# Three of the seven up products with the high and low rows in one 512-column matmul

## The chip, the cores and the metric

The kernel runs on one core of a Trainium2 chip. The metric is device time in microseconds (us): the median of 3 runs for the kernel before. Profiles come from one profiled execution each.

## The reference, cut to what matters

The reference is one decoder block: two mixing branches, and then a gated ConvFFN on 512 tokens. The change touches only the first product of the ConvFFN:

```python
def conv_ffn(h, w_up, conv_w, conv_b, w_down):
    u = h @ w_up                                  # 512 x 2048 @ 2048 x 11264, float32
    ...
    c = up[:, 0:S] * conv_w[0] + up[:, 1:S + 1] * conv_w[1] + up[:, 2:S + 2] * conv_w[2] + conv_b
    val, gate = jnp.split(c, 2, axis=-1)
    return (jax.nn.silu(gate) * val) @ w_down
```

## The kernel before

**Products.** A float32 operand is split into a high part and a low part (type fp32r), and a product is taken as three matmuls: high weights by high rows, high weights by low rows, low weights by high rows. `h @ w_up` is done in 44 blocks `f`. Block `f` gives 128 channels of the value half and 128 of the gate half, for all 512 tokens. It is a 2 by 2 by 2 block product (channel half, half of the 2048 inputs, half of the tokens), done with seven products instead of eight: P1, P2, P7, P6, P5, Q4, P3. Each product multiplies a 1024 x 128 weight tile (a tile of `w_up`, or a sum of such tiles) by 1024 x 256 rows. The rows, sums of quarters of `h`, are prepared once and stay in SBUF as high and low tiles: b11, b21, b22, t1, t2, t3, t4, each 128 x 8 x 256.

**One product (`mm`, L1109).** For each of 8 slices k of the inputs, three matmuls of 256 columns go into one PSUM accumulator (L1124): `whi` by the high rows, `whi` by the low rows, `wlo` by the high rows, so 24 matmuls a product and 168 a block. There are three accumulators a block: X, Y and Z. A PSUM bank holds 512 columns; from block 4 on each accumulator has a bank for itself and uses its first 256 columns. X takes P1, P6, P5, P3, Y takes P7 and Q4, Z takes P2.

**Preparing weights (`load`, `sums`, `parts`).** SyncE loads the tiles, and for some a GpSimd DMA adds a second tile to the one in SBUF (L1093). For P6 and P3 VectorE adds two tiles first (L1100). ScalarE copies the tile to the high part `whi` (L1105), VectorE subtracts it for the low part `wlo` (L1107). The ring for `whi` and `wlo` holds three products.

**Taking out (`out`, L1127).** ScalarE copies X into `u` (L1152) after P1, P6, P5 and P3. VectorE adds Z into `u` after P2 (L1156), Y after Q4 (L1156), and Y after P5 (L1154, behind ScalarE's copy of X).

**Behind it.** `conv` (L1161) puts the convolution, silu and gating into a list `later`: ScalarE L1173 and L1179, VectorE L1176 and L1181. After an odd block VectorE also makes factors for the down product (L884 to L888), and ScalarE issues their stores (L893 to L895).

**Order of the work.** From block 7 on the steps of a block are P7, P6, P2, P5, P1 of the next block, Q4, P3; the last block has P6, P7, P5, P2, Q4, P3. At step i, `run` (L1252) first prepares the weights of step i + 2 with one entry of `later` beside it, then emits the matmuls of step i and then its `out`. All of these instructions are pinned to this order on each engine, and each engine runs its list in order.

Of the kernel before, what the change touches and what calls it, by code (L numbers as in the profile page):

```python
# [8 lines left out]
F32 = mybir.dt.float32  # L9
F32R = mybir.dt.float32r  # L10
# [3 lines left out]
ALU = mybir.AluOpType  # L14
# [4 lines left out]
P = 128  # L19
S = 512  # L20
# [114 lines left out]
def block_kernel(ctx: ExitStack, tc: tile.TileContext, d: Dims, a: dict, out: bass.AP):  # L135
    nc = tc.nc
    act, dve, pool, pe, sync = nc.scalar, nc.vector, nc.gpsimd, nc.tensor, nc.sync
    NK, NP, NQ, NKV, NF = d.NK, d.NP, d.NQ, d.NKV, d.NF
# [16 lines left out]
    NPRE = 4  # L155
# [50 lines left out]
    pin = tc.keep_in_program_order  # L206
# [13 lines left out]
    for f in range(NPRE):  # L220
        w, t = a["w_up"][f], {n: up_d[f, n] for n in ("s3", "s1", "P6", "P3")}
# [70 lines left out]
    if True:  # L292
# [3 lines left out]
        with tc.tile_pool(name="x0_ps", bufs=6, space=PSUM) as ps0:  # L296
# [10 lines left out]
            for h in range(2):  # L307
                hs = slice(h * HT * P, (h + 1) * HT * P)
                for k in range(NK):
                    ps = ps0.tile([P, HT * P], F32, name="ps_x", tag="x")  # L310
# [45 lines left out]
        with ExitStack() as pt:  # L356
# [32 lines left out]
            for t in range(NKV):  # L389
# [12 lines left out]
                ps = small().rearrange("p (n c) -> p n c", c=P)  # L402
                for b in range(NT):
                    pe.transpose(ps[:, b], vf[:, b * P : (b + 1) * P], ident)
                ps = ps.rearrange("p n (h c) -> p n h c", c=HD)
# [14 lines left out]
            for g in range(NHK):  # L420
# [7 lines left out]
                for n in range(NT):  # L428
# [37 lines left out]
                    ps = small()  # L466
# [540 lines left out]

    upx = ExitStack()
    bqp = upx.enter_context(tc.tile_pool(name="bqA", bufs=1, reuse_waits="tile"))
    bq = {n: [bqp.tile([P, KH, TH], F32R, name=f"{n}{i}") for i in range(2)] for n in ("b11", "b21")}  # L1010
    hp = hps.enter_context(tc.tile_pool(name="hhlO", bufs=3, reuse_waits="tile"))
    NCC = d.D // S
    ssp = tcp.tile([P, NT, NCC], F32, name="ssp")
# [62 lines left out]
    us = []  # L1076
    dve.tensor_scalar(cw[:, 0:3, NF:], cw[:, 0:3, NF:], -1.0, None, op0=ALU.mult)

    class Block:

        def __init__(self, f):
            self.f, self.w, self.hl = f, {}, {}
            self.apart = 2 <= f < NPRE

        def load(self, n):
            f, w = self.f, self.w
# [20 lines left out]
        def mm(self, n):  # L1109
            if n == "P1":  # L1110
                x = ups.tile([P, S], F32, name="X", tag="X")
                self.X = x[:, :TH]
                self.Z = x[:, TH:] if self.f < NPRE else upy.tile([P, S], F32, name="Z", tag="Y")[:, :TH]
            if n == "P7":
                self.Y = upy.tile([P, S], F32, name="Y", tag="Y")[:, :TH]
            into = {"P2": "Z", "P7": "Y", "Q4": "Y"}.get(n, "X")
            ps = getattr(self, "Z" if self.apart and n in ("P5", "P3") else into)
            start = n in ("P1", "P7") or n == "P2" and self.f >= NPRE or n == "P5" and self.apart
            whi, wlo = (x.rearrange("p (k c) -> p k c", c=P) for x in self.hl.pop(n))
            xh, xl = bq[{"P1": "b11", "P2": "b21", "P7": "t3", "P6": "t2", "P5": "t1", "Q4": "t4", "P3": "b22"}[n]]  # L1120
            for k in range(KH):
                last = k == KH - 1
                for i, (l, r) in enumerate(((whi, xh), (whi, xl), (wlo, xh))):
                    pin(pe.matmul(ps, l[:, k], r[:, k], start=start and k + i == 0, stop=last and i == 2,  # L1124
                                  skip_group_check=True))

        def out(self, n):  # L1127
            if n == "P7":
                return
            X, Y, Z = self.X, getattr(self, "Y", None), self.Z  # L1130
            if n == "P1" and self.f < NPRE:
                self.t1 = up.tile([P, TH], F32, name="t1", tag="t1", bufs=NPRE)
                pin(act.activation(self.t1, X, AF.Copy))
                return

            if self.f < NPRE:
                if n == "P2":
                    pin(dve.tensor_tensor(self.t1, self.t1, Z, op=ALU.add))
                    return
                if self.apart and n != "P1":  # L1140
                    if n != "P6":
                        i, j, more = {"P5": (1, 1, (Z, Y)), "P3": (0, 1, (Z,)), "Q4": (1, 0, (Y,))}[n]
                        u = us[self.f % 2][:, i, 2 + j * TH : 2 + (j + 1) * TH]
                        pin(act.activation(u, X, AF.Copy))
                        for ps in more:
                            pin(dve.tensor_tensor(u, u, ps, op=ALU.add))
                    return
            i, j, ps, first = {"P1": (0, 0, X, True), "P2": (0, 0, Z, False), "P6": (1, 0, X, True), "P5": (1, 1, X, True),
                               "Q4": (1, 0, Y, False), "P3": (0, 1, X, True)}[n]
            u = us[self.f % 2][:, i, 2 + j * TH : 2 + (j + 1) * TH]  # L1150
            if first:
                pin(act.activation(u, ps, AF.Copy))  # L1152
                if n == "P5":
                    pin(dve.tensor_tensor(u, u, Y, op=ALU.add))  # L1154
            else:
                pin(dve.tensor_tensor(u, u, ps, op=ALU.add))  # L1156

        def place(self):
            pin(act.activation(us[self.f % 2][:, 0, 2 : 2 + TH], self.t1, AF.Copy))
# [137 lines left out]


    bqp = upx.enter_context(tc.tile_pool(name="bqB", bufs=1, reuse_waits="tile"))
    bq.update({n: [bqp.tile([P, KH, TH], F32R, name=f"{n}{i}") for i in range(2)] for n in ("b22", "t1", "t3", "t2", "t4")})  # L1300
    up = upx.enter_context(tc.tile_pool(name="upw", bufs=1, side="left", reuse_waits="tile"))

    psx = ExitStack()
# [180 lines left out]
```

## Time and profile before

| what | value |
| --- | --- |
| median of 3 runs (lowest to highest) | 2802.57 us (2802.53 to 2804.05) |
| the profiled execution's own time | 2802.24 us |
| its span, first to last instruction | 2800.5 us |
| mean granted TensorE clock | 0.998 |
| VectorE busy, whole span | 71% |
| ScalarE busy, whole span | 48% |
| up blocks, first and last matmul start | 1474.6 to about 2376 us of the span |

Engines in the profile: PE is TensorE's matmuls, PEld its weight loads, DVE is VectorE, ACT ScalarE, POOL GpSimd, SP SyncE. L1124 is line 1124 of the kernel. A row of the timeline gives start, duration, engine, line, operation, output<-inputs and count, and in brackets how long the engine sat idle before it and what ended that. Durations of neighbours on one engine overlap, so the spacing of starts tells how long an instruction holds its engine.

### The profile page before, as it was taken

The page shows a single profiled execution, that of the slowest core. Times are in us where ns is not written, and L with a number is a line of the kernel's source. Part 1 is how long each engine was busy: PE and PEld are TensorE (multiplying, and loading weights), DVE is VectorE, ACT ScalarE, POOL GpSimd, SP SyncE. Part 2 cuts the span into 40 slices and gives each one's busy share as a digit, 9 for nine tenths or more (in the row PEclk, how much of TensorE's full clock was granted, in tenths as well). Part 3 has the DMA queues.
Part 4 walks back from the last instruction along what each step waited for, and adds up shares of the span by engine and source line. Part 5 has one row for each costly group of instructions (what it writes and reads, how often), then busy time and mean ns, then how long its engine had stood idle before and what let it go on. Part 6 is the DMA issues. An engine that isn't in the chain of part 4 may idle for free.

```text
span 2800.5 us, 45992 instructions
## 1 busy us (share of the span) xinstructions
PE 2759.3 (99%) x17466; PEld 2400.8 (86%) x17466; DVE 1988.9 (71%) x3452; ACT 1352.9 (48%) x2278; POOL 231.3 (8%) x307
## 2 busy tenths in 40 slices
PE   6999999999999999999999999999999999999999
PEld 5777778787778778888889999999999999888887
DVE  5588677877787774545678778787777778655555
ACT  4255445545544553322465555554555555444444
POOL 0001011110111001011000011101010101000000
PEclk9999999999999999999999999999999999999999
DMA  7865887787778767888776888888898888877775
GB/s 221 226 160 161 210 212 187 189 195 192 186 184 198 183 176 216 243 250 283 252 256 186 233 227 227 243 232 222 232 243 229 225 231 237 319 243 240 257 256 187
DMA packets 227182, 619.62 MB, mean 221 GB/s; under 512 B 24832, under 2 KB 44944, under 8 KB 225936
## 3 DMA queue, kind: packets, MB, share of 16 engines
q1 hardware_dynamic: 158400, 441.03, 48.2%
q0 software_dynamic: 37216, 136.33, 25.7%
q10 hardware_dynamic: 31344, 39.31, 4.1%
q8 instruction: 137, 2.24, 0.3%
q14 instruction: 85, 0.70, 0.1%
HBM read 566.96 MB, written 191.18 MB: 271 GB/s over the span
## 4 chain that ended last, share of the span: by engine, by line
PE 63%; DVE 2%; DMA 1%; ACT 1%; issue 0%; ACTq 0%; DVEq 0%; SPq 0%
PE X L1124 17%; PE X L988 10%; PE Y L988 9%; PE Y L1124 9%; PE acc L270 4%; PE acc L269 4%; PE acc L271 4%; PE Z L1124 4%; DMA raw<-in_w_dn_dram 1%; DVE wlo L1107 0%; DVE c L1176 0%; PE psS L761 0%; ACT whi L1105 0%; PE ps_t L1054 0%; PE psG L752 0%
## 5 line engine op out<-in xcount | busy, mean ns | idle before, releaser
L269 PE MATMUL acc<-xhi,whi 128*128 128x512 f32 x1152 | 462.7, 402 | 1.9 <-DVE xlo L315 1.9
L270 PE MATMUL acc<-xlo,whi 128*128 128x512 f32 x1152 | 459.8, 399 | 0.0
L271 PE MATMUL acc<-xhi,wlo 128*128 128x512 f32 x1152 | 459.5, 399 | 0.0
L254 ACT ACTIVATE whi<-raw 128x512 fp32r<-128x512 f32 x352 | 220.5, 630 | 404.9 <-PE acc L270 326.6
L981 DVE TENSOR_TENSOR wlo<-raw,whi 128x1024 fp32r<-128x1024 f32 x210 | 256.7, 1224 | 199.7 <-ACT whi L980 198.2
L980 ACT ACTIVATE whi<-raw 128x1024 fp32r<-128x1024 f32 x210 | 222.5, 1060 | 282.2 <-PE X L988 131.9
L255 DVE TENSOR_TENSOR wlo<-raw,whi 128x512 fp32r<-128x512 f32 x352 | 241.7, 689 | 162.3 <-ACT whi L254 142.7
L1107 DVE TENSOR_TENSOR wlo<-raw,whi 128x1024 fp32r<-128x1024 f32 x184 | 224.6, 1222 | 77.4 <-ACT whi L1105 77.3
L1124 PE MATMUL X<-b,whi 128*128 128x256 f32 x1472 | 268.9, 283 | 0.2 <-ACT whi L1105 0.2
L1124 PE MATMUL X<-t,whi 128*128 128x256 f32 x1408 | 257.2, 283 | 1.4 <-ACT u L1152 1.4
L1124 PE MATMUL Y<-t,whi 128*128 128x256 f32 x1408 | 257.1, 283 | 0.0
L269 PEld LDWEIGHTS acc<-xhi,whi 128*128 128x128 f32 x1152 | 217.0, 188 | 41.7 <-DVE xlo L315 2.1
L271 PEld LDWEIGHTS acc<-xhi,wlo 128*128 128x128 f32 x1152 | 216.8, 188 | 40.0 <-issue 0.9
L270 PEld LDWEIGHTS acc<-xlo,whi 128*128 128x128 f32 x1152 | 217.0, 188 | 39.4 <-issue 1.7
L1124 PEld LDWEIGHTS X<-b,whi 128*128 128x128 f32 x1472 | 229.6, 192 | 0.5 <-ACT whi L1105 0.4
L1105 ACT ACTIVATE whi<-a 128x1024 fp32r<-128x1024 f32 x124 | 130.9, 1056 | 201.3 <-DVE a L1100 195.9
L1124 PEld LDWEIGHTS X<-t,whi 128*128 128x128 f32 x1408 | 219.6, 192 | 1.6 <-ACT u L1152 1.6
L1124 PEld LDWEIGHTS Y<-t,whi 128*128 128x128 f32 x1408 | 219.6, 192 | 0.0
L1124 PE MATMUL X<-b,wlo 128*128 128x256 f32 x736 | 208.5, 283 | 0.9 <-DVE wlo L1107 0.9
L1105 ACT ACTIVATE whi<-raw 128x1024 fp32r<-128x1024 f32 x184 | 192.9, 1049 | 23.0 <-ACT whi L1105 13.9
L1107 DVE TENSOR_TENSOR wlo<-a,whi 128x1024 fp32r<-128x1024 f32 x124 | 151.9, 1225 | 67.6 <-ACT whi L1105 67.0
L1124 PE MATMUL X<-t,wlo 128*128 128x256 f32 x704 | 199.4, 283 | 0.3 <-DVE wlo L1107 0.3
(387 smaller groups left out, 5796.9 us busy)
## 6 DMA issues: line engine op xcount, KB each, us to landing
raw<-in_w_up_dram SPq DMA_DIRECT2D x170, 512.0 KB
raw<-in_w_z_dram SPq DMA_DIRECT2D x288, 256.0 KB
s_dn<-in_w_dn_dram POOLq DMA_DIRECT2D x88, 512.0 KB, 7.4
raw<-s_dn SPq DMA_DIRECT2D x88, 512.0 KB
raw<-in_w_up_dram POOLq DMA_DIRECT2D x80, 512.0 KB, 8.5
raw<-in_w_dn_dram SPq DMA_DIRECT2D x66, 512.0 KB
s_dn<-in_w_dn_dram SPq DMA_DIRECT2D x44, 512.0 KB
s_dn<-s_dn SPq DMA_DIRECT2D x44, 512.0 KB
```

Of the source, the lines that this page charges most:

```text
L254: act.activation(hi, raw, AF.Copy)
L255: dve.tensor_tensor(lo, raw, hi.bitcast(F32), op=ALU.subtract)
L269: stream.append(pe.matmul(acc, whi[:, j], xhi[:, k], start=first, stop=False))
L270: stream.append(pe.matmul(acc, whi[:, j], xlo[:, k], start=False, stop=False))
L271: stream.append(pe.matmul(acc, wlo[:, j], xhi[:, k], start=False, stop=last))
L980: act.activation(whi, wr, AF.Copy)
L981: dve.tensor_tensor(wlo, wr, whi.bitcast(F32), op=ALU.subtract)
L988: pe.matmul(dst, l[:, q, ts], r[:, es], start=fst and j == 0, stop=lst and j == 2, skip_group_check=True)
L1105: pin(act.activation(hi, t, AF.Copy))
L1107: return lambda: pin(dve.tensor_tensor(lo, t, hi.bitcast(F32), op=ALU.subtract))
L1124: pin(pe.matmul(ps, l[:, k], r[:, k], start=start and k + i == 0, stop=last and i == 2, skip_group_check=True))
```

## The change

High and low rows of one name now lie in one tile (`bqt`), high first. In blocks 7 to 42, the products P7, Q4 and P2 pass both in one matmul of 512 columns: high weights by (high rows, low rows). It writes a whole PSUM bank; the first 256 columns get high by high, the other 256 high by low. `wlo` by the high rows still goes to the first 256 columns. So the low sums of Y and of Z stand in the second half of the bank, and `out` adds them into `u` with one more VectorE add after P5, Q4 and P2 each.

```diff
--- before.py
+++ after.py
@@ -1007,7 +1007,8 @@
 
     upx = ExitStack()
     bqp = upx.enter_context(tc.tile_pool(name="bqA", bufs=1, reuse_waits="tile"))
-    bq = {n: [bqp.tile([P, KH, TH], F32R, name=f"{n}{i}") for i in range(2)] for n in ("b11", "b21")}
+    bqt = {n: bqp.tile([P, 2, KH, TH], F32R, name=n) for n in ("b11", "b21")}
+    bq = {n: [t[:, i] for i in range(2)] for n, t in bqt.items()}
     hp = hps.enter_context(tc.tile_pool(name="hhlO", bufs=3, reuse_waits="tile"))
     NCC = d.D // S
     ssp = tcp.tile([P, NT, NCC], F32, name="ssp")
@@ -1076,13 +1077,16 @@
     us = []
     dve.tensor_scalar(cw[:, 0:3, NF:], cw[:, 0:3, NF:], -1.0, None, op0=ALU.mult)
 
+    WIDE = ("P7", "Q4", "P2")
+
     class Block:
 
 
 
         def __init__(self, f):
-            self.f, self.w, self.hl = f, {}, {}
+            self.f, self.w, self.hl, self.full = f, {}, {}, {}
             self.apart = 2 <= f < NPRE
+            self.wide = WIDE if NPRE + 3 <= f < NF - 1 else ()
 
         def load(self, n):
             f, w = self.f, self.w
@@ -1110,16 +1114,26 @@
             if n == "P1":
                 x = ups.tile([P, S], F32, name="X", tag="X")
                 self.X = x[:, :TH]
-                self.Z = x[:, TH:] if self.f < NPRE else upy.tile([P, S], F32, name="Z", tag="Y")[:, :TH]
+                z = x if self.f < NPRE else upy.tile([P, S], F32, name="Z", tag="Y")
+                self.Z = x[:, TH:] if self.f < NPRE else z[:, :TH]
+                self.full.update(X=x.rearrange("p (e s) -> p e s", e=2), Z=z.rearrange("p (e s) -> p e s", e=2))
             if n == "P7":
-                self.Y = upy.tile([P, S], F32, name="Y", tag="Y")[:, :TH]
+                y = upy.tile([P, S], F32, name="Y", tag="Y")
+                self.Y = y[:, :TH]
+                self.full["Y"] = y.rearrange("p (e s) -> p e s", e=2)
             into = {"P2": "Z", "P7": "Y", "Q4": "Y"}.get(n, "X")
             ps = getattr(self, "Z" if self.apart and n in ("P5", "P3") else into)
             start = n in ("P1", "P7") or n == "P2" and self.f >= NPRE or n == "P5" and self.apart
             whi, wlo = (x.rearrange("p (k c) -> p k c", c=P) for x in self.hl.pop(n))
-            xh, xl = bq[{"P1": "b11", "P2": "b21", "P7": "t3", "P6": "t2", "P5": "t1", "Q4": "t4", "P3": "b22"}[n]]
+            nm = {"P1": "b11", "P2": "b21", "P7": "t3", "P6": "t2", "P5": "t1", "Q4": "t4", "P3": "b22"}[n]
+            xh, xl = bq[nm]
             for k in range(KH):
                 last = k == KH - 1
+                if n in self.wide:
+                    pin(pe.matmul(self.full[into], whi[:, k], bqt[nm][:, :, k], start=start and k == 0, stop=False,
+                                  skip_group_check=True))
+                    pin(pe.matmul(ps, wlo[:, k], xh[:, k], start=False, stop=last, skip_group_check=True))
+                    continue
                 for i, (l, r) in enumerate(((whi, xh), (whi, xl), (wlo, xh))):
                     pin(pe.matmul(ps, l[:, k], r[:, k], start=start and k + i == 0, stop=last and i == 2,
                                   skip_group_check=True))
@@ -1148,12 +1162,16 @@
             i, j, ps, first = {"P1": (0, 0, X, True), "P2": (0, 0, Z, False), "P6": (1, 0, X, True), "P5": (1, 1, X, True),
                                "Q4": (1, 0, Y, False), "P3": (0, 1, X, True)}[n]
             u = us[self.f % 2][:, i, 2 + j * TH : 2 + (j + 1) * TH]
+            adds = [Y] if n == "P5" else []
+            adds += [self.full["Y"][:, 1]] if n in ("P5", "Q4") and "P7" in self.wide else []
+            adds += [self.full["Z"][:, 1]] if n == "P2" and n in self.wide else []
+            adds += [self.full["X"][:, 1]] if n in ("P5", "P3") and n in self.wide else []
             if first:
                 pin(act.activation(u, ps, AF.Copy))
-                if n == "P5":
-                    pin(dve.tensor_tensor(u, u, Y, op=ALU.add))
             else:
-                pin(dve.tensor_tensor(u, u, ps, op=ALU.add))
+                adds.insert(0, ps)
+            for more in adds:
+                pin(dve.tensor_tensor(u, u, more, op=ALU.add))
 
         def place(self):
             pin(act.activation(us[self.f % 2][:, 0, 2 : 2 + TH], self.t1, AF.Copy))
@@ -1297,7 +1315,8 @@
 
 
     bqp = upx.enter_context(tc.tile_pool(name="bqB", bufs=1, reuse_waits="tile"))
-    bq.update({n: [bqp.tile([P, KH, TH], F32R, name=f"{n}{i}") for i in range(2)] for n in ("b22", "t1", "t3", "t2", "t4")})
+    bqt.update({n: bqp.tile([P, 2, KH, TH], F32R, name=n) for n in ("b22", "t1", "t3", "t2", "t4")})
+    bq.update({n: [t[:, i] for i in range(2)] for n, t in bqt.items()})
     up = upx.enter_context(tc.tile_pool(name="upw", bufs=1, side="left", reuse_waits="tile"))
 
     psx = ExitStack()
```

`order` of the built programs shows what this makes on the engines. In all, PE has 864 matmuls fewer (24 in each of 36 blocks) and VectorE 108 adds more; the lists of ScalarE, GpSimd and SyncE hold the same instructions.

PE, the start of P2 in a steady block, before (b_13704 and b_13705 are the high and low rows b21; the brackets name the engines whose semaphore is waited for):

```order
L1124 MATMUL Z<-b_13704,whi 128x256 [waits Activation_49]
L1124 MATMUL Z<-b_13705,whi 128x256
L1124 MATMUL Z<-b_13704,wlo 128x256 [waits DVE_49]
L1124 MATMUL Z<-b_13704,whi 128x256
L1124 MATMUL Z<-b_13705,whi 128x256
L1124 MATMUL Z<-b_13704,wlo 128x256
```

The same place in the change, with one tile b_13703 for both:

```order
L1133 MATMUL Z<-b_13703,whi 128x512 [waits PE_49,Activation_49]
L1135 MATMUL Z<-b_13703,wlo 128x256 [waits DVE_49]
L1133 MATMUL Z<-b_13703,whi 128x512
L1135 MATMUL Z<-b_13703,wlo 128x256
L1133 MATMUL Z<-b_13703,whi 128x512
```

The two matmuls by `whi` became one of 512 columns, so two slices take four rows instead of six. The first also waits for PE's own matmuls into the same bank two blocks earlier.

VectorE, from the output of P2 to the output of P5 in an even block, before (u is the row tile of the block, a the weight sum for P3, c the convolution; the first add is P2's, the second P5's):

```order
L1156 TENSOR_TENSOR u_15587<-u_15587,Z 128x256 [waits PE_49]
L1176 SCALAR_TENSOR_TENSOR c_19545<-u_15589,par,c_19545 128x512 [waits DVE_49]
L1107 TENSOR_TENSOR wlo<-raw,whi 128x1024 [waits DMAHW7_49,Activation_49]
L1154 TENSOR_TENSOR u_15587<-u_15587,Y 128x256 [waits Activation_49]
L1100 TENSOR_TENSOR a_19144<-a_19144,raw 128x1024
L1181 TENSOR_TENSOR c_19545<-c_19545,c_19480 128x512 [waits DVE_49]
L1107 TENSOR_TENSOR wlo<-a_19144,whi 128x1024 [waits PE_49,Activation_49]
```

The same place in the change:

```order
L1174 TENSOR_TENSOR u_15580<-u_15580,Z 128x256 [waits PE_49]
L1174 TENSOR_TENSOR u_15580<-u_15580,Z 128x256 [waits DVE_49]
L1194 SCALAR_TENSOR_TENSOR c_19299<-u_15582,par,c_19299 128x512
L1111 TENSOR_TENSOR wlo<-raw,whi 128x1024 [waits DMAHW7_49,Activation_49]
L1174 TENSOR_TENSOR u_15580<-u_15580,Y 128x256 [waits Activation_49]
L1174 TENSOR_TENSOR u_15580<-u_15580,Y 128x256 [waits DVE_49]
L1104 TENSOR_TENSOR a_18934<-a_18934,raw 128x1024
L1199 TENSOR_TENSOR c_19299<-c_19299,c_19242 128x512
L1111 TENSOR_TENSOR wlo<-a_18934,whi 128x1024 [waits PE_49,Activation_49]
```

An add of Z's second half stands behind the add of Z and one of Y's second half behind the add of Y, each waiting for the add before it (DVE). The sum, the low parts and the convolution follow them.

VectorE a little later, at the output of Q4 in the same block, before:

```order
L885 TENSOR_TENSOR tq<-c_19545,c_19314 128x256 [waits DVE_49]
L1107 TENSOR_TENSOR wlo<-raw,whi 128x1024 [waits DMASW3_49,PE_49,Activation_49]
L1156 TENSOR_TENSOR u_15587<-u_15587,Y 128x256 [waits PE_49]
L1100 TENSOR_TENSOR a_19383<-a_19383,raw 128x1024 [waits DMASW4_49]
L887 SCALAR_TENSOR_TENSOR tq<-tq,c_19545 128x256 [waits DVE_49]
```

And in the change:

```order
L885 TENSOR_TENSOR tq<-c_19299,c_19089 128x256 [waits DVE_49]
L1111 TENSOR_TENSOR wlo<-raw,whi 128x1024 [waits DMASW3_49,PE_49,Activation_49]
L1174 TENSOR_TENSOR u_15580<-u_15580,Y 128x256 [waits PE_49]
L1174 TENSOR_TENSOR u_15580<-u_15580,Y 128x256 [waits DVE_49]
L1104 TENSOR_TENSOR a_19152<-a_19152,raw 128x1024 [waits DMASW4_49]
L887 SCALAR_TENSOR_TENSOR tq<-tq,c_19299 128x256
```

Here too an add of Y's second half stands ahead of the sum for the next block's P6.

## The prediction

> **What bounds the kernel now.** I read the page's busy shares first, then the stage that the change touches, by the windows view, with its columns ahead of it.
>
> ```profile
> PE 2759.3 (99%) x17466; PEld 2400.8 (86%) x17466; DVE 1988.9 (71%) x3452; ACT 1352.9 (48%) x2278; POOL 231.3 (8%) x307
> ```
>
> ```profile
> core 0: us, PE busy (x) PEld busy (x) DVE busy (x) ACT busy (x) POOL busy (x), PEclk, DMA share, GB/s
> 1650.00:2350.00 700.00, 700.00 (x5836) 700.00 (x5835) 550.63 (x659) 358.80 (x487) 75.14 (x87) 1.00 0.86 232
> ```
>
> In the steady up blocks TensorE is never idle, at full clock (1.00); VectorE is busy 550.63 of 700 us, 79%. So removed TensorE time is gained only as long as nothing else becomes late. The waits view of this stretch has no row of PE. Its largest rows of DVE and ACT are these (us in total, times, longest):
>
> ```profile
> ACT whi L1105 <- DVE a L1100: 175.6, 71, 3.4
> DVE wlo L1107 <- ACT whi L1105: 117.5, 156, 1.6
> ACT u L1152 <- PE X L1124: 69.2, 56, 1.9
> ```
>
> Much of VectorE's idle time is spent waiting for ScalarE, which waits for VectorE: sum, high part, low part. That idle time is not free room. It belongs to one chain through both engines, and only waits for PE can shrink when work is added.
>
> **The saving on PE.** The timeline of PE gives both spacings: products of 256 columns, and the down product's 512 columns (19 rows from first to last).
>
> ```profile
> 1608.09 0.28 PE L1124 MATMUL X<-b,wlo 128*128 128x256 f32 x1
> 1608.21 0.40 PE L1124 MATMUL X<-b,whi 128*128 128x256 f32 x2
> 1608.45 0.28 PE L1124 MATMUL X<-b,wlo 128*128 128x256 f32 x1
> ```
>
> ```profile
> 2499.82 0.39 PE L988 MATMUL X<-wlo,hhi 128*128 128x512 f32 x1
> ...
> 2503.90 0.39 PE L988 MATMUL X<-wlo,hhi 128*128 128x512 f32 x1
> ```
>
> Three matmuls in 0.36 us are 120 ns each; 18 spacings in 4.08 us are 226.7 ns each. Two narrow ones become one wide one: 240 - 226.7 = 13.3 ns saved. A block has 3 wide products of 8 such pairs: 24 x 13.3 ns = 0.32 us. In 36 blocks (7 to 42) that is 864 matmuls and 11.5 us. The columns streamed stay the same. A wide matmul whose moving rows lie in two pieces has no row before; bounds are 226.7 ns and the 240 ns of two narrow ones, and I take 226.7; the result below does not hang on it, as PE has 1.8 us to spare over 48 wide matmuls.
>
> **The cost on DVE.** Each wide product leaves 256 columns more to be added: one more add at the output of P5, Q4 and P2, of the form u<-u,PSUM, behind an add into the same u. Such a pair stands in an early block:
>
> ```profile
> 1562.62 0.41 DVE L1146 TENSOR_TENSOR u<-u,X 128x256 f32<-128x256 f32 x1
> 1563.06 0.42 DVE L1146 TENSOR_TENSOR u<-u,Y 128x256 f32<-128x256 f32 x1
> 1563.40 0.42 DVE L884 TENSOR_TENSOR tq<-c 128x256 f32<-128x256 f32 x1
> ```
>
> Two adds hold the engine 0.78 us. A single one holds it 0.33 us (1704.95 to 1705.28 below). So an added add costs 0.45 us: 1.35 us a block, 2.70 us for two blocks.
>
> The Trainium skill ("VectorE: DVE Perf Modes", section "The DRAIN you can't avoid") says that a semaphore between two VectorE instructions costs nothing extra. The rows disagree, 0.44 us to the dependent add against 0.34 us to the independent instruction; what it would make of the time is the third rival.
>
> **Where this lies on the path.** The order of work repeats every two blocks (factors for the down product come with odd blocks): 2 x 168 matmuls x 120 ns = 40.32 us. I followed DVE and ACT from P5 of block 10 to P5 of block 12, 1704.95 to 1745.27, also 40.32 us.
>
> ```profile
> 1704.53 0.38 ACT L1152 ACTIVATE u<-X 128x256 f32<-128x256 f32 x1 [1.89 <-PE X L1124]
> 1704.95 0.42 DVE L1154 TENSOR_TENSOR u<-u,Y 128x256 f32<-128x256 f32 x1 [0.76 <-ACT u L1152]
> 1705.28 1.22 DVE L1100 TENSOR_TENSOR a<-a,raw 128x1024 f32<-128x1024 f32 x1
> 1706.60 1.06 ACT L1105 ACTIVATE whi<-a 128x1024 fp32r<-128x1024 f32 x1 [1.68 <-DVE a L1100]
> 1707.56 0.37 ACT L1152 ACTIVATE u<-X 128x256 f32<-128x256 f32 x1
> 1709.50 1.22 DVE L1107 TENSOR_TENSOR wlo<-raw,whi 128x1024 fp32r<-128x1024 f32 x1
> 1710.63 0.41 DVE L1156 TENSOR_TENSOR u<-u,Y 128x256 f32<-128x256 f32 x1
> 1720.04 1.22 DVE L1107 TENSOR_TENSOR wlo<-raw,whi 128x1024 fp32r<-128x1024 f32 x1 [1.65 <-ACT whi L1105]
> ```
>
> ```profile
> 1721.85 0.28 PE L1124 MATMUL X<-t,wlo 128*128 128x256 f32 x1
> ```
>
> VectorE is tied to PE at 1704.95: it waited for ACT's copy, which waited for the end of P5. From there to the low part of P5 of block 11 (1720.04, ended 1721.26) every wait is between DVE and ACT. PE uses that low part at 1721.85, so the tightest product has 0.59 us in hand. On this way lie the new adds of P5 and Q4 of block 10, 0.90 us, while PE arrives 3 x 0.107 = 0.32 us earlier (Q4, P7, P2). So it is 0.63 us short: **PE stalls**. Q4's new wait for the second add of P5 (done near 1705.8) is covered by P1; Q4 starts at 1707.21.
>
> Does the delay vanish before the next odd block? In the second half of the pair these are the waits for PE that can give way:
>
> ```profile
> 1724.10 1.22 DVE L1107 TENSOR_TENSOR wlo<-raw,whi 128x1024 fp32r<-128x1024 f32 x1
> 1725.24 0.41 DVE L1154 TENSOR_TENSOR u<-u,Y 128x256 f32<-128x256 f32 x1
> 1729.19 1.23 DVE L1107 TENSOR_TENSOR wlo<-raw,whi 128x1024 fp32r<-128x1024 f32 x1
> 1730.45 0.42 DVE L1156 TENSOR_TENSOR u<-u,Y 128x256 f32<-128x256 f32 x1
> 1743.29 1.22 DVE L1107 TENSOR_TENSOR wlo<-raw,whi 128x1024 fp32r<-128x1024 f32 x1
> 1745.27 0.42 DVE L1154 TENSOR_TENSOR u<-u,Y 128x256 f32<-128x256 f32 x1 [0.76 <-ACT u L1152]
> ```
>
> ```profile
> 1732.12 1.06 ACT L1105 ACTIVATE whi<-a 128x1024 fp32r<-128x1024 f32 x1 [2.97 <-DVE a L1100]
> 1733.33 0.39 ACT L1152 ACTIVATE u<-X 128x256 f32<-128x256 f32 x1
> 1737.86 1.04 ACT L1105 ACTIVATE whi<-raw 128x1024 fp32r<-128x1024 f32 x1
> 1739.09 0.38 ACT L1152 ACTIVATE u<-X 128x256 f32<-128x256 f32 x1 [0.19 <-PE X L1124]
> ```
>
> A low part followed by an add takes 1.13 us without a wait (1709.50 to 1710.63); 1724.10 to 1725.24 is the same, so DVE is late already in odd blocks now. 1729.19 to 1730.45 has 0.13 us more, 1743.29 to 1745.27 0.85 us more. On ACT a high part followed by a copy takes 0.96 us (1706.60 to 1707.56); the two here take 1.21 and 1.23 us, 0.25 and 0.27 us more, and DVE's next low parts hang on what follows them. Together 0.13 + 0.25 + 0.27 + 0.85 = 1.50 us can give way.
>
> So the chain of two blocks, with no wait for PE left, takes 40.32 - 1.50 + 2.70 = 41.52 us. PE alone needs 40.32 - 0.64 = 39.68 us. The chain is longer: **DVE and ACT set the pace**, PE's saving is waited away, and two blocks take 1.20 us more than now. From the first tied wide block to the last there are 17 pairs, with the ends at most 18: 20.4 to 21.6 us. I take 20.5, as the first pair also uses up what is in hand.
>
> The sum is against the profiled execution: span 2800.5 us, with what lies around it 2802.24 us; 2802.24 + 20.5 = 2822.7. The median of the runs is 0.33 us above that execution: **2823.0 us**.
>
> Bounds: with an add at the 0.33 us of a lone one, two blocks take 40.32 - 1.50 + 1.98 = 40.80 us, 0.48 more, about 8 us in all: 2811. With only the two waits of DVE giving way, not ACT's, 40.32 - 0.98 + 2.70 = 42.04 us, 1.72 more, 30 us: 2832. The value taken goes by the rows of dependent adds. Everything else costs nothing on the path: the merged tiles hold the same bytes and the lists of SP and POOL have the same transfers; PE's new waits on matmuls two blocks back were met long before. Wide PSUM tiles take no more banks.
>
> **Rivals.** First, faster: VectorE's 21% idle time takes the adds in and PE stays the bound. Then the saving shows: 2802.57 - 11.5 = 2791. For it: busy 79% plus 1.35 us in 20.16 is only 86%. Against it: the 0.59 us before P5. Chance 0.08. The Trainium skill ("TensorE: Matmul & The Clock Gate", section "Back-to-back issue gap") gives N/2.4 + 2.5 ns at full clock, by which a pair saves about 2.6 ns, an estimate, and this rival would end near 2800; the rows' 120 and 226.7 ns give 13.3.
>
> Second, about the same: DVE catches up in each even block, and only P5 of 17 odd blocks stalls. How a stall looks:
>
> ```profile
> 1572.84 1.23 DVE L1107 TENSOR_TENSOR wlo<-raw,whi 128x1024 fp32r<-128x1024 f32 x1 [0.20 <-ACT whi L1105]
> ```
>
> ```profile
> 1574.12 0.39 PE L1124 MATMUL Z<-b,wlo 128*128 128x256 f32 x1 [0.76 <-DVE wlo L1107]
> 1574.34 0.40 PE L1124 MATMUL Z<-b,whi 128*128 128x256 f32 x2
> ```
>
> PE goes on 0.05 us after the low part's end (1574.07), and the next matmul follows after 0.22 instead of 0.12 us. So 0.63 + 0.05 + 0.10 = 0.78 us each, 13.3 us, against 11.5 saved: 2804. It needs 1.35 us of adds plus the lag to fit in the even block's 1.50 us. Chance 0.12.
>
> Third, the added adds cost 0.33 us, as the bound above: 2811, slower still. Against it stands the dependent pair. Chance 0.06.
>
> Fourth, slower than the forecast: only DVE's waits give way, 2832 and above. Chance 0.07 above the range. That the change doesn't do what it says is excluded by the order of the built program, where 864 matmuls are gone and 108 adds have come.
>
> **How the numbers follow.** Forecast 0.67, the rivals 0.08, 0.12, 0.06 and 0.07. The range takes in the second and third rival and the upper bound: 2803 to 2832; it leaves out 0.15. About 0.2%, 5.6 us, is what a measurement of this kernel can tell from no change: faster than 2797 has 0.08, up to 2808 0.12, slower 0.80.
>
> **What would show it.** In the profile after: PE below 100% in the steady blocks, with waits for DVE's low parts at P5 of odd blocks and some at P2, P3 or P6; VectorE's add of Y at P5 no longer waiting 0.76 us for ACT; two blocks in about 41.5 us; wide matmuls 227 ns apart where PE runs. A steady stage with no PE wait and 39.7 us per pair would make the prediction wrong, and so would stalls at P5 alone.

## The result, and the profile after

The changed kernel takes **2812.1 us**, the median of seven runs (2809.32 to 2813.6), and the kernel before, on the same chip, 2802.63 us (seven runs, 2799.93 to 2804.05). The ratio is 1.003, with a 95% interval of 1.002 to 1.004: 9.5 us slower. The direction is the predicted one and the time lies in the range, but the loss is less than half of the forecast 20.5 us. The profiled execution took 2809.32 us, 7.1 us more than that of before, with a span of 2807.5 us.

The page's line of busy times is this:

```profile
PE 2765.2 (98%) x16602; PEld 2358.0 (84%) x16602; DVE 2028.0 (72%) x3560; ACT 1347.3 (48%) x2278; POOL 231.5 (8%) x307
```

864 matmuls are gone and 108 instructions of VectorE have come. In the stretch of the steady up blocks the windows view gives:

```profile
core 0: us, PE busy (x) PEld busy (x) DVE busy (x) ACT busy (x) POOL busy (x), PEclk, DMA share, GB/s
1650.00:2350.00 700.00, 698.61 (x4957) 651.99 (x4956) 584.02 (x757) 348.43 (x480) 75.11 (x87) 1.00 0.86 230
```

TensorE now has gaps, at an unchanged clock. The waits view of the same stretch (us in total, times, longest):

```profile
ACT whi L1109 <- DVE a L1104: 226.9, 69, 3.9
DVE wlo L1111 <- ACT whi L1109: 108.3, 120, 1.6
ACT u L1170 <- PE X L1138: 52.9, 34, 1.8
PEld X L1138 <- DVE wlo L1111: 8.8, 37, 0.4
```

There is a row of TensorE (its weight loads) that before had none. ScalarE waits 55 us longer for VectorE's sums, which the adds now precede; in this stretch its row before was the following (the three rows of the waits view that the prediction shows are of a stretch 10 us longer, up to 2360):

```profile
ACT whi L1105 <- DVE a L1100: 171.7, 69, 3.4
```

The stalls themselves stand in the timeline of PE, at the third matmul of P6 and of P3 in block 11, the first that uses the low part:

```profile
1716.26 0.40 PE L1138 MATMUL X<-t,whi 128*128 128x256 f32 x2
1716.73 0.39 PE L1138 MATMUL X<-t,wlo 128*128 128x256 f32 x1
1716.95 0.40 PE L1138 MATMUL X<-t,whi 128*128 128x256 f32 x2
...
1730.97 0.40 PE L1138 MATMUL X<-b,whi 128*128 128x256 f32 x2
1731.36 0.39 PE L1138 MATMUL X<-b,wlo 128*128 128x256 f32 x1
1731.59 0.40 PE L1138 MATMUL X<-b,whi 128*128 128x256 f32 x2
```

Without a stall the low matmul starts 0.24 us behind the first row and the next one 0.12 us behind it. Here it is 0.47 and 0.22, and 0.39 and 0.23 us. Over the blocks 10 to 41 P6 of an odd block takes 3.21 us (mean of 16) instead of 2.88, P3 3.13 and P5 2.99; in even blocks no product is longer by more than 0.01 us on the average.

The pace is read from VectorE's first add of Y at P5 in blocks 10, 11 and 12, in the timeline of DVE:

```profile
1706.09 0.87 DVE L1174 TENSOR_TENSOR u<-u,Y 128x256 f32<-128x256 f32 x2
1706.88 1.22 DVE L1104 TENSOR_TENSOR a<-a,raw 128x1024 f32<-128x1024 f32 x1
...
1726.89 0.87 DVE L1174 TENSOR_TENSOR u<-u,Y 128x256 f32<-128x256 f32 x2
...
1745.63 1.22 DVE L1111 TENSOR_TENSOR wlo<-raw,whi 128x1024 fp32r<-128x1024 f32 x1
1746.77 0.41 DVE L1174 TENSOR_TENSOR u<-u,Y 128x256 f32<-128x256 f32 x1
```

The two adds (x2; the window of this view ends behind the first of the last pair) hold VectorE 0.79 us, near the 0.78 of the prediction. Two blocks take 40.68 us: 20.80 from the even to the odd block and 19.88 back. Before, the same adds stood at 1704.95, 1725.24 and 1745.27: 20.29 and 20.03. **So the second half gained 0.15 us although 1.35 us of adds came, that is, 1.50 us gave way, the sum of the prediction. In the first half 0.84 us gave way, where the prediction had none.** The four waits of the second half that the prediction listed did give way: the last low part and the add behind it, for one, are 1.14 us apart now (1745.63 to 1746.77), against 1.98 before.

The place of the 0.84 us is ScalarE's queue between two blocks. There the program has, in this order: the high part for P6, the copy of P3's output, the three stores of the factors (L893 to L895), the next convolution's first step. The timeline of ACT before (ACTq rows are the issues of the stores):

```profile
1712.30 1.06 ACT L1105 ACTIVATE whi<-a 128x1024 fp32r<-128x1024 f32 x1 [3.42 <-DVE a L1100]
1713.18 0.34 ACTq L893 DMA_DIRECT2D h_dn<-c  x1
1713.26 0.37 ACT L1152 ACTIVATE u<-X 128x256 f32<-128x256 f32 x1
1713.56 0.50 ACTq L894 DMA_DIRECT2D h_dn<-c  x1
1714.15 0.51 ACTq L895 DMA_DIRECT2D h_dn<-tq  x1
1714.71 0.82 ACT L1173 ACTIVATE c<-u,par 128x512 f32<-128x512 f32 x1 [1.08 <-DVE wlo L1107]
```

and after:

```profile
1714.36 1.06 ACT L1109 ACTIVATE whi<-a 128x1024 fp32r<-128x1024 f32 x1 [3.89 <-DVE a L1104]
1714.40 0.34 ACTq L893 DMA_DIRECT2D h_dn<-c  x1
1714.78 0.47 ACTq L894 DMA_DIRECT2D h_dn<-c  x1
1715.32 0.37 ACT L1170 ACTIVATE u<-X 128x256 f32<-128x256 f32 x1
1715.35 0.51 ACTq L895 DMA_DIRECT2D h_dn<-tq  x1
1715.90 0.82 ACT L1191 ACTIVATE c<-u,par 128x512 f32<-128x512 f32 x1 [0.22 <-issue]
```

After, the first store is issued 0.04 us behind the start of the high part: the queue runs ahead of the unit. Before, it is issued only 0.88 us behind it, because the copy ahead of it in the queue waits for P3, whose last matmul ends at 1713.13 on TensorE (the row of PE):

```profile
1712.85 0.28 PE L1124 MATMUL X<-b,wlo 128*128 128x256 f32 x1
```

From the first store to the convolution's step it takes the same 1.5 us in both. So before, the convolution's step was tied to the end of P3, through a wait in the queue that the idle times don't show, as the unit was still busy with the high part. From the high part to the step it was 2.41 us before and is 1.54 now: 0.87 us was a wait for TensorE. The rest of the first half grew by what was added: 0.92 us from the add of Y to this high part (two adds), 0.46 us from the step to the next add of Y (one add); 0.92 - 0.87 + 0.46 is the 0.51 us by which it is longer. Over the 17 such places, behind the even blocks 8 to 40, the way from the high part to the step is 2.41 us before and 1.57 after on the average, 0.84 us less.

### The profile page after: what moved, and what is told of

The parts are those of the page before. It is cut to its first block, busy times and chain, and to the rows that moved or that the text cites. A ratio compares the mean times of both kernels' runs of the same rounds, so it can differ in the third digit from the quotient of the medians.

```text
span 2807.5 us, 44476 instructions
## 1 busy us (share of the span) xinstructions
PE 2765.2 (98%) x16602; PEld 2358.0 (84%) x16602; DVE 2028.0 (72%) x3560; ACT 1347.3 (48%) x2278; POOL 231.5 (8%) x307
## 4 chain that ended last, share of the span: by engine, by line
PE 53%; DVE 8%; ACT 3%; issue 2%; DMA 1%; ACTq 0%; POOL 0%; SPq 0%; DVEq 0%; POOLq 0%
PE X L1138 12%; PE X L988 11%; PE Y L988 9%; PE acc L270 4%; PE acc L271 4%; PE acc L269 4%; DVE wlo L1111 3%; PE Y L1133 2%; ACT whi L1109 2%; PE Z L1133 2%; DVE a L1104 2%; PE Y L1135 1%; PE Y L1138 1%; DVE u L1174 1%; PE Z L1135 1%
## 5 line engine op out<-in xcount | busy, mean ns | idle before, releaser
L1133 PE MATMUL Y<-t,whi 128*128 128x512 f32 x576 | 206.9, 399 | 0.0
L988 PE MATMUL X<-whi,hhi 128*128 128x512 f32 x480 | 187.1, 390 | 0.7 <-ACT u L1170 0.7
```

The lines of the kernel that those rows point to most:

```text
L988: pe.matmul(dst, l[:, q, ts], r[:, es], start=fst and j == 0, stop=lst and j == 2, skip_group_check=True)
L1133: pin(pe.matmul(self.full[into], whi[:, k], bqt[nm][:, :, k], start=start and k == 0, stop=False, skip_group_check=True))
```

## The experiments

Times are medians; each ratio is against the kernel before on the same chip, which took 2802.63 us beside the changed kernel, 2804.64 beside e1 to e4, 2804.59 beside e6 to e9 and 2804.01 beside e10 to e13. The pace is worked out from the starts of P7 in blocks 10 and 40 in each trace, 15 pairs apart.

| kernel | wide products | two blocks, us | time, us | ratio (95%) |
|---|---|---|---|---|
| before | none | 40.32 | 2802.63 | |
| changed | 3 | 40.71 | 2812.1 | 1.003 (1.002 to 1.004) |
| e1: adds left out | 3 | 40.02 | 2799.36 | 0.998 (0.9971 to 0.9989) |
| e2: adds alone | none | 40.72 | 2812.3 | 1.0026 (1.0017 to 1.0036) |
| e3: two wide | 2 | 40.14 | 2802.22 | 0.9993 (0.9983 to 1.0002) |
| e4: stores later | 3 | 40.39 | 2802.06 | 0.9989 (0.998 to 0.9998) |
| e6: two wide, stores later | 2 | 40.11 | 2797.42 | 0.997 (0.996 to 0.998) |
| e7: e6, rows side by side | 2 | 40.11 | 2797.02 | 0.9972 (0.996 to 0.9983) |
| e8: e4, rows side by side | 3 | 40.35 | 2802.74 | 0.9993 (0.9984 to 1.0001) |
| e9: e1, rows side by side | 3 | 40.01 | 2798.04 | 0.9976 (0.9967 to 0.9985) |
| e10: e6, wide matmuls first | 2 | 39.97 | 2794.68 | 0.9966 (0.9953 to 0.9978) |
| e11: second adds later | 3 | 40.34 | 2803.54 | 1.0 (0.9991 to 1.0009) |
| e12: e11, wide first, stores later | 3 | 39.80 | 2792.26 | 0.9958 (0.9945 to 0.9972) |
| e13: before, stores later | none | 40.32 | 2801.02 | 0.9988 (0.9979 to 0.9997) |

**The matmuls without the adds, and the adds without the matmuls.** The edit of e1 takes out of the output step

```
-            adds += [self.full["Y"][:, 1]] if n in ("P5", "Q4") and "P7" in self.wide else []
-            adds += [self.full["Z"][:, 1]] if n == "P2" and n in self.wide else []
-            adds += [self.full["X"][:, 1]] if n in ("P5", "P3") and n in self.wide else []
```

> This kernel has the wide matmuls but leaves out the 108 added adds, so the products of the high rows with the low rows that stand in the second half banks are missing from its output. Theory (one chain through VectorE and ScalarE sets the pace of the changed kernel, with no wait for PE in it: 40.71 us for two blocks): without the adds the chain takes 40.71 - 6 x 0.45 = 38.0 us, TensorE needs 40.32 - 6 x 0.0485 = 40.03 us by the 2.832 us that a wide product takes in the changed kernel's trace; TensorE sets the pace again, no stall in the steady blocks, 36 x 0.146 = 5.2 us saved: about 2797.4 us. By the saving that the prediction took (13.3 ns a pair) it would be 11.5 us: 2791. Rival (the wide matmuls themselves, not the adds, make the kernel slower): 2805 or more.

The edit of e2, on the kernel before, for blocks 7 to 42:

```
                     pin(dve.tensor_tensor(u, u, Y, op=ALU.add))
+                    if 7 <= self.f < NF - 1:
+                        pin(dve.tensor_tensor(u, u, Y, op=ALU.add))
             else:
                 pin(dve.tensor_tensor(u, u, ps, op=ALU.add))
+                if 7 <= self.f < NF - 1:
+                    pin(dve.tensor_tensor(u, u, ps, op=ALU.add))
```

> The kernel before with narrow matmuls, and with three adds more in each of blocks 7 to 42: the add of Y at P5, of Y at Q4 and of Z at P2 is done twice, so these sums are counted twice in its output. Theory (the chain of VectorE and ScalarE sets the pace and holds no wait for PE): the same chain as in the changed kernel, so about 40.7 us for two blocks and the same time as the changed kernel within 2 us, 2809 to 2813, though TensorE has all its matmuls back; TensorE's stalls in two blocks come to 0.39 instead of 0.69 us. Rival (each add costs its share and the wide matmuls give their saving back beside it): the changed kernel's +9.5 plus the 5.2 us that the wide matmuls save, 2817.

Without the adds the time falls by 5.3 us and the pace to 40.0 us: TensorE sets it, and the wide matmuls save 0.32 us in two blocks, 6.7 ns a pair of matmuls instead of 13.3. With the adds alone the pace is that of the changed kernel, 40.7 us, though TensorE has all its matmuls back. Its adds at P5 of blocks 10, 11 and 12, in the timeline of DVE:

```profile
1706.64 0.41 DVE L1154 TENSOR_TENSOR u<-u,Y 128x256 f32<-128x256 f32 x1
...
1727.41 0.41 DVE L1154 TENSOR_TENSOR u<-u,Y 128x256 f32<-128x256 f32 x1
...
1747.28 0.41 DVE L1154 TENSOR_TENSOR u<-u,Y 128x256 f32<-128x256 f32 x1
```

20.77 and 19.87 us, 40.64 together, against 20.80 and 19.88. The loop of VectorE and ScalarE runs at its own length; what TensorE saves or doesn't save beside it makes no difference. The rival's 2817 falls.

**One add less in each block.** e3 makes only two products wide:

```
-    WIDE = ("P7", "Q4", "P2")
+    WIDE = ("P7", "Q4")
```

> P7 and Q4 wide, P2 narrow: two added adds in a block instead of three. Theory (the longer of two chains counts): VectorE and ScalarE need 40.71 - 2 x 0.45 = 39.81 us for two blocks, TensorE 40.32 - 4 x 0.0485 = 40.13 us, so TensorE sets the pace and its saving shows: 72 x 0.0485 = 3.5 us, about 2799. Rival (each add costs its share): two thirds of the changed kernel's 9.5 us, about 2809.

40.11 us in most pairs of blocks and 2.4 us less than before, where 3.5 was expected and the interval touches no change. Two of the seventeen pairs from block 8 on are longer, by 0.50 and 0.18 us, at P5 of an odd block. Two thirds of the adds cost almost nothing, so the loss isn't proportional to the adds: it begins where the loop becomes longer than TensorE's work.

**The stores out of the loop.** e4 moves one line of the convolution steps of the changed kernel, so that the stores stand where ScalarE waits for a sum:

```
-            if part == 0 and f and f % 2 == 0:
+            if part == 4 and f and f % 2 == 0:
                 B[f - 1].keep()
```

> The changed kernel with all three products wide; only the three stores of the factors on ScalarE's queue stand later, at the next even block's fifth conv step, where ScalarE waits for VectorE's sum. Theory (the stores' issues lie on the chain: 1.69 us from the high part to the next conv's first step, of which the high part and the copy alone need 1.28): the chain shortens by 0.41 us to 40.30 us for two blocks, against TensorE's 40.03; 17 x 0.41 = 7.0 us less than the changed kernel, about 2803 to 2805. Rival (the stores lie beside the chain, ScalarE has idle time enough): unchanged, about 2812.

The time goes from 9.5 us above before to 2.6 us below. The timeline of ACT at the place that held the stores:

```profile
1716.15 1.06 ACT L1109 ACTIVATE whi<-a 128x1024 fp32r<-128x1024 f32 x1 [3.88 <-DVE a L1104]
1717.12 0.37 ACT L1170 ACTIVATE u<-X 128x256 f32<-128x256 f32 x1
1717.38 0.81 ACT L1191 ACTIVATE c<-u,par 128x512 f32<-128x512 f32 x1
```

The convolution's step starts 1.23 us behind the high part instead of 1.54, and most pairs of blocks take 40.33 us, as expected (40.30). So the issues of the stores did lie in the loop.

e13 is the control, the same move in the kernel before.

> The kernel before with the three stores later and nothing else changed. Theory (TensorE sets the pace of before at 40.32 us for two blocks, and the stores lie in a chain that is shorter): no change, within 2 us of before. Rival (the place of the stores is worth time by itself, by their transfers): 3 us or more less than before.

The steady pace stays at 40.32 us, as the theory has it, but the kernel is 3.0 us faster (0.8 to 5.9 by the interval), 1 us more than the theory allowed: the rival's number came, though not in the steady blocks. Its trace has 1.3 us less from the first up matmul to P7 of block 10 (216.85 against 218.19), and 1.4 us less from the last up matmul to the end (423.82 against 425.22). So 2 to 3 us of the times with later stores come from outside the steady blocks, and e4 and e6, whose traces have the same two short stretches, are below what their pace gives. Which step there gains was not followed further.

**Two wide products with the stores later.**

> P7 and Q4 wide, P2 narrow, and the three stores later. Theory: the chain of VectorE and ScalarE is 40.33 us for two blocks with three added adds and later stores, so 40.33 - 0.90 = 39.43 us with two; TensorE needs 40.11 us, as in the kernel with two wide products, and sets the pace: 17 x 0.21 = 3.6 us less than before, and the single stalls at P5 of an odd block that stood in that kernel are gone, as the chain has 0.7 us in hand. Rival (the stores matter beyond the chain, by their transfers): another time than 3 to 5 us below before.

The pace is 40.11 us in sixteen of seventeen pairs and no product is stalled at P5 any more. 7.2 us less than before is more than expected; the pace gives 3.6, and the move of the stores outside the steady blocks about 3, as e13 showed.

**What the wide matmul costs.** A wide and a narrow matmul take 354 ns together, against 226.7 + 120 = 346.7. The two pieces of the moving rows were the first suspect. e7, e8 and e9 put high and low rows of one k side by side (cut to what matters; the second group of rows and the code that fills them change alike):

```
-    bqt = {n: bqp.tile([P, 2, KH, TH], F32R, name=n) for n in ("b11", "b21")}
-    bq = {n: [t[:, i] for i in range(2)] for n, t in bqt.items()}
+    bqt = {n: bqp.tile([P, KH, 2, TH], F32R, name=n) for n in ("b11", "b21")}
+    bq = {n: [t[:, :, i] for i in range(2)] for n, t in bqt.items()}
...
-                    pin(pe.matmul(self.full[into], whi[:, k], bqt[nm][:, :, k], start=start and k == 0, stop=False,
+                    pin(pe.matmul(self.full[into], whi[:, k], bqt[nm][:, k], start=start and k == 0, stop=False,
```

> As the kernel with two wide products and later stores, but high and low rows of one k stand side by side, so the 512 moving columns are one piece of 2048 bytes instead of two pieces of 1024 bytes that lie apart. Theory (the two pieces cost the 7.3 ns by which a wide and a narrow matmul, 354 ns, exceed 226.7 + 120): a wide product takes 8 x 346.7 ns = 2.773 us, two blocks 40.32 - 4 x 0.107 = 39.89 us, which the chain (39.43) allows: 7.7 us less than before, about 4 us less than with the pieces apart. Rival (the alternation of 512 and 256 columns costs it, not the pieces): 2.83 us a wide product still, the same time as the kernel with the pieces apart.

> Three wide products, later stores, rows side by side. Theory (the longer of two chains counts): TensorE needs 39.68 us for two blocks if the pieces cost the 7.3 ns, but VectorE and ScalarE still need 40.33 us: the same time as with the pieces apart, within 1 us of before's time, and the shorter matmuls are waited away at P6 of the odd blocks. Rival (TensorE's saving shows at once): 5 us less than the kernel with later stores.

> Three wide products, rows side by side, stores where they were, and the added adds left out, so the products of the high rows with the low rows that stand in the second half banks are missing from its output. Theory: the chain without the adds is about 38 us for two blocks, TensorE sets the pace at 40.32 - 6 x 0.107 = 39.68 us if the pieces cost the 7.3 ns: 36 x 0.32 = 11.5 us less than before, the saving that the prediction took, and 6 us less than the same kernel with the pieces apart. Rival (the alternation costs it): 5.2 us less than before.

This theory fell: in all three a wide product still takes 2.832 us, and the times are those of the kernels with the pieces apart. Pieces 1024 bytes long cost nothing here. Only what e8 was to show of the loop came out: 40.35 us, the pace of VectorE and ScalarE in e4 (40.39).

e10 then changes the order inside a wide product: eight wide matmuls, and behind them eight narrow ones.

> P7 and Q4 wide, later stores, rows in two pieces, and in each wide product first the eight wide matmuls and then the eight narrow ones, instead of wide and narrow in turn. Theory (the turn from 512 to 256 columns and back costs the 7.3 ns of a pair, since the pieces don't): equal matmuls follow each other at 226.7 and 120 ns, a wide product takes 8 x 346.7 ns = 2.773 us, two blocks 39.89 us: 7.7 us less than before, 4 us less than the same kernel in turns. Rival (a wide matmul costs 234 ns in these blocks whatever stands beside it): 2.83 us a wide product and 40.11 us for two blocks, as in turns.

The timeline of PE in the changed kernel, in turns, and then in e10 (eight of a kind in a row):

```profile
1694.48 0.40 PE L1133 MATMUL Y<-t,whi 128*128 128x512 f32 x1
1694.72 0.28 PE L1135 MATMUL Y<-t,wlo 128*128 128x256 f32 x1
1694.84 0.40 PE L1133 MATMUL Y<-t,whi 128*128 128x512 f32 x1
```

```profile
1692.34 2.00 PE L1133 MATMUL Y<-t,whi 128*128 128x512 f32 x8
1694.18 1.12 PE L1140 MATMUL Y<-t,wlo 128*128 128x256 f32 x8
1695.13 0.40 PE L1137 MATMUL X<-t,whi 128*128 128x256 f32 x2
```

In groups the wide ones take 1.84 us, 230 ns each, and the narrow ones 0.95 us, 119 ns each: 2.79 us instead of 2.83. The pace is 39.97 us, 10.9 ns saved a pair. So the turns between the two widths cost the greater part, though grouping doesn't take off all of it: 2.773 was expected, and 0.02 us a product remain. In the trace this remainder lies on the first five wide matmuls of a product (228 to 236 ns from start to start); behind them 227 ns is reached. The change of weights from `whi` to `wlo` is not the cost by itself: the narrow products change them too, at 120 ns.

**The same adds at another place.** e11 leaves all adds in the changed kernel, and puts the second of each pair behind VectorE's next sum or convolution step:

```
-            for more in adds:
-                pin(dve.tensor_tensor(u, u, more, op=ALU.add))
+            for e, more in enumerate(adds):
+                put = lambda more=more: pin(dve.tensor_tensor(u, u, more, op=ALU.add))
+                behind.append(put) if e else put()
...
                 pin(dve.tensor_tensor(t, t, w["s1" if n == "P6" else "a12"], op=ALU.add))
+                flush()
...
             some_later(1)
+            flush()
             lo = B[f].parts(nm)
```

> The changed kernel with all its matmuls and adds; only the second add of each pair stands later: behind VectorE's sum a<-a,raw at P5 and Q4, where VectorE then waits 0.4 to 0.6 us for ScalarE, and behind the next conv step at P2. Theory (the adds cost time by their place ahead of the sum on which ScalarE's high part waits, not by their number): the chain falls from 40.71 by 3 x 0.45 + 0.42 at P5 and Q4 and 2 x 0.11 at P2 to about 38.7 us, TensorE (40.00) sets the pace: 5.4 us less than before, as without the adds. Rival (VectorE's work counts, wherever it stands): 40.7 us for two blocks and 7 to 9 us more than before.

Neither number came: the pace is 40.34 us and the time that of before. The stalls at P6, P5 and P3 are gone, so the place of the adds does count. But a new wait has come, at Q4 of odd blocks. First the timeline of DVE, then of PE:

```profile
1726.14 0.42 DVE L1181 TENSOR_TENSOR u<-u,Y 128x256 f32<-128x256 f32 x1
1726.47 1.22 DVE L1110 TENSOR_TENSOR a<-a,raw 128x1024 f32<-128x1024 f32 x1
1727.61 0.41 DVE L1181 TENSOR_TENSOR u<-u,Y 128x256 f32<-128x256 f32 x1
1727.94 0.68 DVE L1207 TENSOR_TENSOR c<-c,c 128x512 f32<-128x512 f32 x1
```

```profile
1727.84 0.28 PE L1145 MATMUL X<-b,wlo 128*128 128x256 f32 x1
1728.17 0.47 PE L1140 MATMUL Y<-t,whi 128*128 128x512 f32 x1
```

Q4 writes into the bank that the second add still reads, and waits for VectorE's semaphore. The add ends at 1728.02, Q4 starts at 1728.17 instead of 1727.96. P1 and the wait behind it take 3.18 us (mean) instead of 2.88. These rows also show the price of a dependent add: placed apart, the second add holds VectorE 0.33 us; right behind the add that it waits for it makes the pair 0.45 us longer than one add.

**All together.** e12 has three wide products, wide matmuls first, second adds later and stores later.

> Three wide products, wide matmuls first and narrow ones behind them, second adds later, stores later. Theory: TensorE sets the pace at 40.32 - 6 x 0.107 = 39.68 us for two blocks if the turns cost the 7.3 ns, with the chain at about 38.3 us: 11.5 us less than before, the whole saving that the prediction took for TensorE. Rival (turns don't cost it): 40.0 us and 5.4 us less.

2792.26 us, 11.7 us less than before on the same chip and some 20 less than the changed kernel: the fastest version found. The pace is 39.80 us with TensorE never idle in the steady blocks; 40.32 - 39.80 = 0.52 us in two blocks is 9.4 us in 36 blocks, and the other 2.3 us are of the size that the control showed outside these blocks. Three edits come together here; what each gives in this kernel was not measured. The wait of e11 doesn't come back. The timeline of DVE in block 11, where Q4 starts at 1724.73:

```profile
1722.47 0.42 DVE L1182 TENSOR_TENSOR u<-u,Y 128x256 f32<-128x256 f32 x1 [0.34 <-ACT u L1178]
1722.81 1.22 DVE L1110 TENSOR_TENSOR a<-a,raw 128x1024 f32<-128x1024 f32 x1
1723.94 0.41 DVE L1182 TENSOR_TENSOR u<-u,Y 128x256 f32<-128x256 f32 x1
```

VectorE is early enough to wait for P5's copy again, and the second add is done 0.38 us ahead of Q4.

## Why the prediction was wrong in its size

**The mechanism held.** VectorE and ScalarE set the pace, and TensorE's saving is waited away. e2 shows it: the same pace without the saving. In the changed kernel's rows no wait for TensorE is left in the loop from P5 to P5, in either half.

**The failed step is the sentence "From there to the low part of P5 of block 11 every wait is between DVE and ACT".** It was read from the idle times of the two units. On ScalarE's queue the copy of P3's output waited for TensorE, with the three stores and the convolution's step behind it. 0.84 us of the loop was such a wait and gave way. The prediction's own mark of a wait, more than 0.96 us from a high part to the copy behind it, finds nothing at this place (1712.30 to 1713.26 is 0.96): the copy was let go (1713.13) shortly before the unit came free, and only the stores and the step behind it came late. With the 0.84 us of ScalarE's own rows the chain is 40.32 - 1.50 - 0.84 + 2.70 = 40.68 us instead of 41.52; the pace measured over 15 pairs is 40.71. Over 17 pairs the error is 17 x 0.81 = 13.8 us, which accounts for the distance between the 2822.7 of the sum and the 2809.32 of the profiled execution (13.4 us). The sign could have been seen: the stores' issue at 1713.18 stands 0.05 us behind the end of P3.

**The saving on PE** was 13.3 ns a pair in the prediction and is 6.7 in the turns of the changed kernel (e1), 10.9 in groups (e10). The upper bound named for the wide matmul, 240 ns, held (236). As the prediction said, the result did not hang on it. By the rule of the Trainium skill that it weighed ("TensorE: Matmul & The Clock Gate", section "Back-to-back issue gap"), which the page gives for an isolated matmul, a pair would save 2.5 ns, 2.2 us for 864 pairs by an estimate. e1 measured 5.3 us.

**The cost on DVE** was right: 0.79 us for two adds in the trace after, 0.45 for the added one. By the rule of the Trainium skill ("VectorE: DVE Perf Modes", section "The DRAIN you can't avoid") that a semaphore between two of its instructions costs nothing extra, both places of the add would cost the same. e11 measured 0.33 us for the add apart from its partner, against 0.45 behind it. In e11's trace the add placed apart still waits on VectorE's semaphore, which was met before: it is the wait that isn't yet met that costs about 0.1 us. The third rival, which took 0.33, gives a time near the result, 2811, by luck: its cause is not the one found.

**P5 of odd blocks** was named as the main place of the stalls, with some at P2, P3 or P6. It is one of three, and the smallest: P6 0.33, P3 0.25 and P5 0.11 us a pair of blocks. Once the loop is the longer one, TensorE meets it at each low part that comes late, and P6 comes first behind the long way through the stores. The sum over the pair is what the loop fixes: 0.71 us of stalls (0.01 of it in even blocks) less 0.32 of TensorE's saving are the 0.39 us by which two blocks are longer.

**The second half of the pair** was right: taken one by one, the four waits that it listed are shorter by 0.12, 0.25, 0.28 and 0.84 us, 1.49 together, against 1.50 in the sum. **The count of pairs** was right: from P7 of block 8 to P7 of block 42 the changed kernel loses 6.6 us in 17 pairs, and behind that 0.8 us in the last blocks.

The measured 9.5 us are about 2 us more than the 7.1 that the profiled executions differ by. The runs of the changed kernel reach from 2809.32 to 2813.6, and the profiled one is the fastest of them; what makes the others longer is open. e2, with the same loop, measured 7.7.

## What to carry to other kernels

An engine's queue can wait while its unit is busy; such a wait, here 0.84 us in two blocks, has no row among the idle times. Ahead of calling a chain closed, compare the time of each issue behind a waiting instruction with the end of what that instruction waits for. And where an added instruction costs time, try its place before its number: in e12 the 108 adds left TensorE without a gap, with the second one behind the sum that another engine waits for and the stores out of the loop; in e11, with the adds moved alone, two blocks still took 0.32 us more than in e1, without them.

## What was not expected of the hardware

Matmuls of 512 and 256 columns in turn take 354 ns a pair (236 behind a wide one, 117 behind a narrow one), against 226.7 and 120 ns among their own kind; in groups of eight the loss shrinks from 0.06 to 0.02 us a product. Moving rows in two pieces of 1024 bytes cost the same as one of 2048. From the first of three issues of stores on ScalarE's queue to the convolution's step behind them it takes 1.4 to 1.9 us (mean 1.53 in the trace before and in the one after), whether the unit is still busy at the first issue, as after, or nearly free, as before.
